# Layer 0 of a hybrid encoder: gated-convolution group first in the last weight piece, long convolution split between ScalarE and VectorE, short-convolution group in split products

## The chip, the cores and the metric

The kernel runs on one core of one Trainium2 chip. The metric is the device time of one execution in microseconds (us); the median of three runs is compared. The engines are named as the profile names them: PE (TensorE matmul), PEld (TensorE weight load), DVE (VectorE), ACT (ScalarE), POOL (GpSimd) and SP (SyncE, which issues nearly all the transfers).

## The reference, cut to what matters

Two layers over 256 positions with 2048 channels. Each layer normalises its input, modulates it with a scale and a shift that come from a conditioning row times `w_mod`, and multiplies by one wide matrix `w_in`. The columns of the product feed four head groups; their outputs go through `w_out`. A gated feed-forward follows. All is float32.

```python
h = layer_norm(x) * (1.0 + scale_m) + shift_m
proj = h @ w_in[l]                                     # 2048 x 4288
uv, q_c, kv_c, k_r, sb, sc, sh, ag = jnp.split(proj, IN_SPLITS, axis=-1)
y_a = gmlp_mixer(uv, ...)                              # U and V columns
y_b = mla_mixer(q_c, kv_c, k_r, ...)                   # B columns, attention
y_c = sb * causal_dwconv(sc * sh, sconv_w[l])          # E columns (sb), C columns (sc, sh), width 3
a, g = jnp.split(ag, 2, axis=-1)                       # D columns
y = causal_dwconv(a * sigmoid(g), conf_w_dw, conf_b_dw)   # width 31, per channel
y_d = silu(layer_norm(y, ...))
y = jnp.concatenate([y_a, y_b, y_c, y_d], axis=-1) @ w_out[l]
```

## The kernel before

**Storage.** Activations lie channel-major: four blocks of 128 channels by 256 positions make a tile of 128x1024. `hF` holds the modulated input of layer 0 in plain float32, one `slot` tile for every 4 of the 16 k-tiles. `hT` holds the same input split in two parts (high part and rest, `split`, L477 to L480), one tile of pool `act` (10 buffers) for every 2 k-tiles. In layer 0 `hT` exists for k-tiles 4 to 15 only (`PLAIN_KT` is 4).

**Products.** A product is either exact or split. Exact: the float32 weights are loaded straight into the split buffers (`wexact`, L438) and multiplied with `hF`; PE runs each such matmul as two instructions. Split: the weights go to a raw buffer (`wraw`, L446; pool `raw` has 4 buffers of 1 MB, used by the modulation weights `wmod` as well), ACT rounds them (`whi`, L460) and DVE subtracts (`wlo`, L461). `chan_major` and `group` then need three matmuls for each block of 128 output channels; `group2` (L533) needs two, one 512 wide (`whi` with both parts of the input) and one 256 wide (`wlo` with the high part).

**Layer 0.** `by_pieces` (L1271) goes over the k-tiles in five pieces, (0,2), (2,2), (4,4), (8,4), (12,4), because the modulation of a piece has to be there first. In each piece the work runs in four quarters: a quarter of D (1024 columns, four PSUM banks that stay open over all pieces, split products from k-tile 4 on), then U, then another quarter of D, V, D, E, D. U, V and E (512 columns each, exact) use two PSUM banks each per piece and are added to `sumU`, `sumV` and `sumE`, three tiles of pool `act`. After the last piece come `mix_d` (sigmoid and product, which starts the long convolution), `mix_u`, `gelu_v`, `mix_v`, then group B (704 columns, exact, `latent_group`), whose end is the attention (`mix_b`), then group C (1024 columns, exact, `group`), whose end is `mix_c`, the short convolution and `mix_e`. `out_proj` multiplies by `w_out`: the first 1024 columns split, the other two chunks of 512 exact.

**The long convolution** (`conv_d`, L890) is a list of 124 steps, one for each of four blocks and 31 taps: the first tap of a block on ACT, the other 30 as one DVE instruction each (L896: product with a tap and addition, up to 256 wide). The steps wait in `background`; `STEPS` says how many are issued with each unit of weights (7 with a unit of B, 8 with one of C). `norm_d` follows the last.

**The modulation stream.** `mods` (L338) yields 16 steps for each of ten rows of modulation, each a load of 1 MB of `w_mod` into a raw buffer and one DVE instruction 2048 wide (L240, the first of a row L238). `RATES` says how many steps are issued with each unit: 1.3 in B, 1.6 in C, 2.1 in `out_proj`. The first row (16 steps) is needed when the first chunk of `out_proj` ends; the second and third (48 steps in all) are needed inside its last chunk, before the second half of the positions.

**Order.** The framework's scheduler places the instructions of each engine when the kernel is built; program order is the priority, and an instruction whose operands or buffers aren't free yet lets later ones pass. At run time each engine goes through its list in order. Attention has a long chain of small steps, and PE works on C between them.

Of the kernel before, what the change touches and what calls it, by code (L numbers as in the profile page):

```python
# [7 lines left out]
F32 = mybir.dt.float32  # L8
F32R = mybir.dt.float32r
AF = mybir.ActivationFunctionType  # L10
ALU = mybir.AluOpType
# [21 lines left out]


RATES = [
    dict(B=1.3, C=1.6, out=2.1, up=0.7, down=0.7),
    dict(D=1.0, U=0.0, V=0.0, B=0.0, C=0.0, E=0.9, out=0.6, up=0.3, down=0.7),
]

STEPS = [  # L40
    dict(B=7, C=8, up=2),
    dict(U=7, B=4, C=4, E=8, up=2),
]

# [6 lines left out]
def encoder_kernel(ctx: ExitStack, tc: tile.TileContext, A: dict, consts: bass.AP, out: bass.AP):  # L51
# [321 lines left out]
    def phase(l, name):  # L373
        pace["rate"] = RATES[l][name]
# [470 lines left out]
    def mixers(l, w_in, Y, hF=None, between=None):  # L845
# [44 lines left out]
        def conv_d(glu):  # L890
            yd = slot("convD").rearrange("p (j s) -> p j s", j=4)
            def tap(j, k):
                if k == 30:
                    ident_act(yd[:, j, :], glu[:, j, :], CW(30, j), CB(j))
                else:
                    dve.scalar_tensor_tensor(  # L896
                        out=yd[:, j, 30 - k :],
                        in0=glu[:, j, : S - 30 + k],
                        scalar=CW(k, j),
                        in1=yd[:, j, 30 - k :],  # L900
                        op0=ALU.mult,
                        op1=ALU.add,
                    )

            for j in range(4):
                for k in range(30, -1, -1):
                    background.append(lambda j=j, k=k: tap(j, k))
            background.append(lambda: norm_d(yd))

        def norm_d(yd):  # L910
# [335 lines left out]
                dve.tensor_tensor(out=c, in0=c, in1=t, op=ALU.mult)  # L1246

        if hF is not None:
            return by_pieces(l, w_in, hF, between, mix_d, mix_u, gelu_v, mix_v, mix_b, mix_c, mix_e)
        phase(l, "V")  # L1250
        first_group(w_in, C_UV + 512, gelu_v)
        phase(l, "D")
# [15 lines left out]
        run(group2(w_in, C_SB, f"E{l}", joined_e, bg=STEPS[l]["E"]))  # L1268
        drain_background()

    def by_pieces(l, w_in, hF, between, mix_d, mix_u, gelu_v, mix_v, mix_b, mix_c, mix_e):  # L1271
# [8 lines left out]
        cols = {"U": C_UV, "V": C_UV + 512, "E": C_SB}  # L1280

        hT[:] = [None] * (PLAIN_KT // 2) + [act_pair("hT") for _ in range((KT - PLAIN_KT) // 2)]

        def terms(kt, part):

            hi, lo = part
            if lo is None:
                return [(hi, hf(kt))]
            xh, xl = (h[:, kt % 2, :] for h in hT[kt // 2][:2])
            return [(hi, xh), (hi, xl), (lo, xh)]  # L1290

        def chan_major(ps, kt, part, blocks, first, last):
            ts = terms(kt, part)
            for i in blocks:
                o = ps[i // 2][:, (i % 2) * S : (i % 2 + 1) * S]
                for n, (w, x) in enumerate(ts):
                    mm(o, w[:, i * P : (i + 1) * P], x, first and n == 0 and i % 2 == 0, last and n == len(ts) - 1)

        def side(g, parts, k0, nkt):
            ps = [acc_tile(f"{g}{l}_{i}") for i in range(2)]  # L1300
            for kt, part in parts:
                st, sp = kt == k0, kt == k0 + nkt - 1
                if g == "V":
                    ts = terms(kt, part)
                    for t in range(2):
                        for n, (w, x) in enumerate(ts):
                            mm(ps[t], x[:, t * P : (t + 1) * P], w, st and n == 0, sp and n == len(ts) - 1)
                else:
                    chan_major(ps, kt, part, range(4), st, sp)
            for i in range(2):  # L1310
                if k0 == 0:
                    act.copy(sums[g][i], ps[i])
                elif k0 + nkt == KT:
                    dve.tensor_tensor(out=sums[g][i], in0=ps[i], in1=sums[g][i], op=ALU.add)
                else:
                    part = tmp_tile("part")
                    act.copy(part, ps[i])
                    dve.tensor_tensor(out=sums[g][i], in0=part, in1=sums[g][i], op=ALU.add)

        first = between(0)[1]  # L1320
        first()
        for q, (k0, nkt) in enumerate(PIECES):
            ahead = between(q + 1) if q + 1 < len(PIECES) else ([], None)
            exact = k0 < PLAIN_KT
            loaded = {}

            def load(g, kt):

                c0, width = (C_AG, 1024) if g == "D" else (cols[g], 512)
                nk = min(2048 // width, nkt)  # L1330
                for j, p in enumerate(weights(w_in, kt, nk, c0, width, exact or g != "D")):
                    loaded[(g, kt + j)] = p

            mods_left = list(ahead[0])
            units = len(mods_left)

            def some_mods(share):
                while mods_left and (units - len(mods_left)) < units * share:
# [36 lines left out]
        run(group(w_in, C_SC, 1024, f"C{l}", mix_ce, hF=hf, bg=STEPS[l]["C"]))  # L1375
        drain_background()


# [253 lines left out]
```

## Time and profile before

| | |
|---|---|
| median of 3 runs | 2281.82 us (2278.19 to 2283.77) |
| the profiled execution | 2273.86 us |
| its span in the profile | 2271.7 us |
| mean granted PE clock | 0.992 |
| PE busy | 2206.6 us (97%) |
| DVE busy | 1792.9 us (79%) |
| ACT busy | 1060.8 us (47%) |
| data moved | 604.10 MB, mean 266 GB/s |

The times in the trace count from the start of the span. In layer 0 the last piece begins at about 157 us, B at 189.7, C has its first matmul at 230.3 and its last at 327.1, and `out_proj` runs from 327.1 to about 443. Layer 1 has its own B at 1292.6 and its own C, in two `group2` runs called Cc and Ch, from 1326.9 to 1402. A row of a list of groups gives the line, engine, operation, output and inputs, shapes and count, then the busy time and the mean of one, then the idle time of the engine ahead of it and what ended it. In a timeline merged rows count several instructions, and the time given reaches to the end of the last one, so the distance between instructions is read from the start of one row to the start of the next.

### The profile page before, as it was taken

What the parts mean: (1) busy time and instruction counts of PE and PEld (TensorE: products, weight loads), DVE (VectorE), ACT (ScalarE), POOL (GpSimd) and SP (SyncE); (2) the same over time, 40 slices, a digit from 0 to 9 for tenths busy, and PEclk for the clock granted to TensorE, in tenths of its full rate; (3) what the DMA queues carried; (4) which work ended last, traced back from release to release, by engine and by line L of the source; (5) the groups of instructions that cost most, each with busy time, mean ns of one, the idle gap of its engine ahead of it and who ended that gap; (6) DMA issues with size and microseconds to landing.
All of it is one profiled execution on the core that took longest, in us unless ns stands there. A gap on an engine that the chain in (4) does not pass through costs nothing. (4 is left out here: it accounts for less than half of the span.)

```text
span 2271.7 us, 28947 instructions
## 1 busy us (share of the span) xinstructions
PE 2206.6 (97%) x11118; PEld 1817.5 (80%) x11118; DVE 1792.9 (79%) x2282; ACT 1060.8 (47%) x1573; POOL 38.9 (2%) x61
## 2 busy tenths in 40 slices
PE   5899999999999999999999999999999999999998
PEld 4686786478888888887886888877888888888886
DVE  6878899588989898998977997878766565565676
ACT  2231241355554554544556544555555454454553
POOL 2000000000000000000000000000000000000000
PEclk9999999999999999999999999999999999999999
DMA  9999889879898989988975765876675555555553
GB/s 349 368 336 322 319 282 388 312 259 330 304 339 303 328 307 330 324 315 294 333 269 191 240 194 181 318 256 209 240 240 181 191 185 189 195 192 187 197 191 148
DMA packets 228658, 604.10 MB, mean 266 GB/s; under 512 B 14548, under 2 KB 27076, under 8 KB 206756
## 3 DMA queue, kind: packets, MB, share of 16 engines
q1 hardware_dynamic: 227672, 601.25, 75.0%
q8 instruction: 87, 1.43, 0.2%
q0 software_dynamic: 848, 1.01, 0.1%
q14 instruction: 51, 0.42, 0.1%
HBM read 600.11 MB, written 2.10 MB: 265 GB/s over the span
## 5 line engine op out<-in xcount | busy, mean ns | idle before, releaser
L461 DVE TENSOR_TENSOR wlo<-wraw,whi 128x1024 fp32r<-128x1024 f32 (+1 forms) x624 | 748.0, 1212 | 299.1 <-ACT whi L460 292.7
L460 ACT CAST whi<-wraw 128x1024 fp32r<-128x1024 f32 (+1 forms) x624 | 648.9, 1046 | 710.9 <-PE g_c L79 189.9
L79 PE MATMUL v_c<-hT,whi 128*128 128x512 f32 x1408 | 490.5, 392 | 0.0
L79 PE MATMUL g_c<-hT,whi 128*128 128x512 f32 x1280 | 445.6, 392 | 0.0
L79 PE MATMUL v_c<-hT,wlo 128*128 128x256 f32 x1408 | 393.9, 280 | 0.0
L79 PE MATMUL d<-whi,a 128*128 128x512 f32 x1344 | 386.8, 389 | 0.0
L240 DVE SCALAR_TENSOR_TENSOR macc<-wmod,cact,macc 128x2048 f32<-128x2048 f32 x150 | 351.6, 2344 | 17.0 <-DMA wmod<-in_w_mod_dram 16.2
L79 PE MATMUL g_c<-hT,wlo 128*128 128x256 f32 x1280 | 358.0, 280 | 0.0
L79 PEld LDWEIGHTS v_c<-hT,whi 128*128 128x128 f32 x1408 | 263.5, 187 | 58.8
L79 PEld LDWEIGHTS d<-whi,a 128*128 128x128 f32 x1344 | 252.1, 188 | 52.3
L79 PEld LDWEIGHTS g_c<-hT,whi 128*128 128x128 f32 x1280 | 239.5, 187 | 53.3
L79 PEld LDWEIGHTS v_c<-hT,wlo 128*128 128x128 f32 x1408 | 265.9, 189 | 0.2
L79 PEld LDWEIGHTS g_c<-hT,wlo 128*128 128x128 f32 x1280 | 241.7, 189 | 0.2
L79 PE MATMUL d<-wlo,a 128*128 128x512 f32 x672 | 233.2, 389 | 1.9 <-DVE wlo L461 1.9
L79 PEld LDWEIGHTS d<-wlo,a 128*128 128x128 f32 x672 | 126.1, 188 | 28.7 <-DVE wlo L461 2.7
L79 PE MATMUL o<-whi,a 128*128 128x512 f32 x352 | 101.1, 394 | 2.5 <-ACT whi L460 2.5
L896 DVE SCALAR_TENSOR_TENSOR convD<-gluD,pm,convD 128x255 f32<-128x255 f32 (+27 forms) x240 | 98.7, 456 | 0.4
L479 ACT CAST a<-g 128x512 fp32r<-128x512 f32 x132 | 81.1, 616 | 33.6 <-PE d L79 30.3
L480 DVE TENSOR_TENSOR a<-g,a 128x512 fp32r<-128x512 f32 x132 | 87.6, 683 | 1.8 <-ACT a L479 1.8
L604 PE MATMUL first<-wexact,hN 128*128 128x512 f32 x192 | 85.7, 596 | 1.5 <-ACT hN L82 1.2
L240 DVE SCALAR_TENSOR_TENSOR qacc<-wmod,cact,qacc 128x1024 f32<-128x1024 f32 (+1 forms) x75 | 80.2, 1070 | 2.4 <-DMA wmod<-in_w_mod_dram 0.4
L79 PEld LDWEIGHTS o<-whi,a 128*128 128x128 f32 x352 | 66.6, 190 | 17.1 <-ACT whi L460 2.9
(353 smaller groups left out, 2431.9 us busy)
## 6 DMA issues: line engine op xcount, KB each, us to landing
wraw<-in_ffn_w_up_dram SPq DMA_DIRECT2D x168, 1024.0 KB, 5.2
wmod<-in_w_mod_dram SPq DMA_DIRECT2D x160, 1024.0 KB, 6.9
wraw<-in_ffn_w_down_dram SPq DMA_DIRECT2D x88, 1024.0 KB, 5.2
wmod<-in_w_mod_dram SPq DMA_DIRECT2D x64, 512.0 KB, 8.8
wraw<-in_w_in_dram SPq DMA_DIRECT2D x30, 1024.0 KB, 6.5
wexact<-in_w_in_dram SPq DMA_DIRECT2D x52, 512.0 KB, 7.0
wraw<-in_w_out_dram SPq DMA_DIRECT2D x24, 1024.0 KB, 7.1
wexact<-in_w_out_dram SPq DMA_DIRECT2D x16, 512.0 KB, 11.4
```

The source lines that it names most:

```text
L79: pe.matmul(o, lhsT, rhs, start=start, stop=stop, skip_group_check=True)
L240: i = dve.scalar_tensor_tensor(out=acc, in0=w, scalar=col, in1=acc, op0=ALU.mult, op1=ALU.add)
L460: held(act.copy(hi[:, :m], r), "cast")
L461: i = dve.tensor_tensor(out=lo[:, :m], in0=r, in1=hi[:, :m].bitcast(F32), op=ALU.subtract)
L479: act.copy(hi, src)
L480: dve.tensor_tensor(out=lo, in0=src, in1=hi.bitcast(F32), op=ALU.subtract)
L604: i = pe.matmul(ps, hN[kt // 4][:, kt % 4, t * P : (t + 1) * P], parts[kt], start=kt == 0, stop=kt == KT - 1, skip_group_check=True,)
L896: dve.scalar_tensor_tensor(out=yd[:, j, 30 - k :], in0=glu[:, j, : S - 30 + k], scalar=CW(k, j), in1=yd[:, j, 30 - k :], op0=ALU.mult, op1 ...
```

## The change

In layer 0 alone: in the last piece all of D comes first, then `mix_d`, then U, V and E, with one step of a new rate `last` and five steps of the convolution behind each. A convolution step is now a whole tap: four ACT products 256 wide into one of two `scaled` tiles (pool `act`), and one DVE addition over all four blocks; 31 steps in place of 124, five behind each of U, V and E and one with each unit of B and C. `hT` is made for k-tiles 0 to 3 too, after `mix_v`. Group C becomes two `group2` runs of 512 columns (four units of 1 MB each) with layer 1's `first_c` (which adds the two halves of the PSUM banks into `chC`) and `second_c` behind them. `sumE` ends in a `slot` tile.

```diff
-    dict(B=1.3, C=1.6, out=2.1, up=0.7, down=0.7),
+    dict(last=1.0, B=1.3, C=1.4, out=2.0, up=0.7, down=0.7),
...
-    dict(B=7, C=8, up=2),
+    dict(last=5, B=1, C=1, up=2),
...
+            scaled = []
+
+            def taps(k):
+                if k == 30:
+                    for j in range(4):
+                        tap(j, k)
+                    return
+                if len(scaled) < 2:
+                    scaled.append(actp.tile([P, 1024], F32, tag="act", name="scaled").rearrange("p (j s) -> p j s", j=4))
+                t, n = scaled[(29 - k) % 2], S - 30 + k
+                for j in range(4):
+                    act.activation(out=t[:, j, :n], in_=glu[:, j, :n], func=AF.Copy, scale=CW(k, j))
+                dve.tensor_tensor(out=yd[:, :, 30 - k :], in0=yd[:, :, 30 - k :], in1=t[:, :, :n], op=ALU.add)
+
+            if hF is not None:
                 for k in range(30, -1, -1):
-                    background.append(lambda j=j, k=k: tap(j, k))
+                    background.append(lambda k=k: taps(k))
+            else:
+                for j in range(4):
+                    for k in range(30, -1, -1):
+                        background.append(lambda j=j, k=k: tap(j, k))
...
+                    if g == "E" and i == 0:
+                        whole = slot("sumE")
+                        ends[:] = [whole[:, j * 512 : (j + 1) * 512] for j in range(2)]
+                    dve.tensor_tensor(out=ends[i] if g == "E" else sums[g][i], in0=ps[i], in1=sums[g][i], op=ALU.add)
...
+            if q == len(PIECES) - 1:
+                for kt, h in turns_d:
+                    d_part(kt, h)
+                mix_d(accD, None)
+                phase(l, "last")
+                for g in "UVE":
+                    load(g, k0)
+                    side(g, [(kt, loaded[(g, kt)]) for kt in range(k0, k0 + nkt)], k0, nkt)
+                    pump()
+                    for _ in range(STEPS[l]["last"]):
+                        background.pop(0)()
+                continue
...
-        mix_d(accD, None)
         mix_u(sums["U"], None)
         for t in range(2):
             gelu_v(t, sums["V"][t])
         mix_v()
+        for i in range(PLAIN_KT // 2):
+            hT[i] = act_pair("hT")
+            split(hT[i], hF[i // 2][:, 2 * (i % 2) : 2 * (i % 2) + 2, :])
...
-        def mix_ce(cps, tps):
-            mix_c(cps, tps)
-            mix_e(sums["E"], None)
+        def mix_ce(cps):
+            second_c(cps)
+            mix_e(ends, None)
 
-        run(group(w_in, C_SC, 1024, f"C{l}", mix_ce, hF=hf, bg=STEPS[l]["C"]))
+        run(group2(w_in, C_SC, f"Cc{l}", first_c, bg=STEPS[l]["C"]))
+        run(group2(w_in, C_SC + 512, f"Ch{l}", mix_ce, bg=STEPS[l]["C"]))
```

More of the change, by code (lines that the diff above doesn't have):

```diff
@@ L903, in tap @@
                     )
-            for j in range(4):
-                for k in range(30, -1, -1):
-                    background.append(lambda j=j, k=k: tap(j, k))
+            scaled = []
[11 more added lines that the diff above has]
+            if hF is not None:
+                for k in range(30, -1, -1):
+                    background.append(lambda k=k: taps(k))
[3 more added lines that the diff above has]
+                        background.append(lambda j=j, k=k: tap(j, k))
             background.append(lambda: norm_d(yd))
@@ L1248, in mixers @@
         if hF is not None:
-            return by_pieces(l, w_in, hF, between, mix_d, mix_u, gelu_v, mix_v, mix_b, mix_c, mix_e)
+            return by_pieces(l, w_in, hF, between, mix_d, mix_u, gelu_v, mix_v, mix_b, first_c, second_c, mix_e)
         phase(l, "V")
@@ L1269, in mixers, with by_pieces @@
         drain_background()
-    def by_pieces(l, w_in, hF, between, mix_d, mix_u, gelu_v, mix_v, mix_b, mix_c, mix_e):
+    def by_pieces(l, w_in, hF, between, mix_d, mix_u, gelu_v, mix_v, mix_b, first_c, second_c, mix_e):
         hf = lambda kt: hF[kt // 4][:, kt % 4, :]
@@ L1280, in by_pieces @@
         cols = {"U": C_UV, "V": C_UV + 512, "E": C_SB}
+        ends = []
         hT[:] = [None] * (PLAIN_KT // 2) + [act_pair("hT") for _ in range((KT - PLAIN_KT) // 2)]
@@ L1313, in side @@
                 elif k0 + nkt == KT:
-                    dve.tensor_tensor(out=sums[g][i], in0=ps[i], in1=sums[g][i], op=ALU.add)
+                    if g == "E" and i == 0:
+                        whole = slot("sumE")
+                        ends[:] = [whole[:, j * 512 : (j + 1) * 512] for j in range(2)]
+                    dve.tensor_tensor(out=ends[i] if g == "E" else sums[g][i], in0=ps[i], in1=sums[g][i], op=ALU.add)
                 else:
```

## The prediction

> **What bounds the kernel now.** First the strips of the profile's page, for the place of the change: 40 slices of 56.8 us, in tenths. Layer 0's group work is slices 3 to 8.
>
> ```profile
> span 2271.7 us, 28947 instructions
> ...
> PE   5899999999999999999999999999999999999998
> ...
> DVE  6878899588989898998977997878766565565676
> ACT  2231241355554554544556544555555454454553
> ...
> DMA  9999889879898989988975765876675555555553
> ```
>
> PE is full from slice 2 on and ACT is the one idle engine there; DVE and the transfers are close behind PE. Strips can't say which of the three is last, so the second view is the table of stretches, cut where the stages change: last piece, B, attention with C, split part of the output projection, exact part.
>
> ```profile
> core 0: us, PE busy (x) PEld busy (x) DVE busy (x) ACT busy (x) POOL busy (x), PEclk, DMA share, GB/s
> 157.00:190.00 33.00, 33.00 (x184) 27.38 (x183) 17.84 (x15) 4.63 (x6) 0.00 (x0) 1.00 0.93 326
> 190.00:230.00 40.00, 39.60 (x143) 25.56 (x142) 37.97 (x72) 7.91 (x17) 1.92 (x2) 1.00 0.92 312
> 230.00:327.00 97.00, 92.67 (x431) 76.30 (x430) 87.14 (x145) 26.86 (x59) 4.64 (x4) 0.98 0.84 309
> 327.00:382.00 55.00, 50.90 (x227) 40.45 (x225) 50.33 (x47) 18.60 (x25) 0.00 (x0) 0.97 0.91 340
> 382.00:430.00 48.00, 47.35 (x129) 22.50 (x129) 31.39 (x26) 2.56 (x8) 0.00 (x0) 1.00 1.03 404
> sum 273.00, PE 263.51 PEld 192.20 DVE 224.67 ACT 60.57 POOL 6.55; mean PE 52.70 PEld 38.44 DVE 44.93 ACT 12.11 POOL 1.31
> ```
>
> PE misses 4.3 us of the 97 in the C stretch; DVE is at 95% in B and 90% with C, but at 54% in the last piece. So PE bounds, and DVE has its room in the wrong place. The Trainium skill warns of this reading ("Trainium Kernel Development and Optimization", Performance Expectations): matmul busy time is a bad measure, weight-load time a good one. By it PE would have slack (76.30 of 97 us), and fewer matmuls need save nothing (that outcome lies in the first rival). The distance of matmuls settles it; here C in layer 0, in the timeline and by tile, and layer 1's second half of C:
>
> ```profile
> 299.91 7.07 PE L79 MATMUL C_c<-hF,wexact 128*128 128x256 f32 x32
> 306.82 1.02 PE L79 MATMUL ps_gate<-macc,ones 128*128 128x512 f32 x2
> L79 PE MATMUL C_c<-hF,wexact x256: 379/379/634, 230.3 to 327.1; 128*128 128x256 f32 x128
> L79 PE MATMUL Ch_c<-hT,whi x64: 390/391/392, 1380.2 to 1402.0; 128*128 128x512 f32 x64
> L79 PE MATMUL Ch_c<-hT,wlo x64: 280/280/280, 1380.4 to 1402.3; 128*128 128x256 f32 x64
> ```
>
> 32 instructions take 306.82 - 299.91 = 6.91 us, one every 0.216 us with no gap: PE's own pace, so here its time is real. The split form takes (1402.0 - 1380.2) / 63 = 0.346 us for a pair, also without gaps.
>
> **The change part by part.**
>
> *C in split products (PE).* 16 k-tiles by 8 blocks are 128 products. Before: 256 x 0.216 = 55.3 us. After: 128 x 0.346 = 44.3 us. **-11.0 us** on the bounding engine, if the weights are there in time. D, U, V, E and B keep their matmuls; D first merely reorders them. D's last two k-tiles are wanted some 6 us into the piece; their buffers are no longer behind U's in the order, so I add nothing.
>
> *The cover.* C fills PE in the gaps of attention. In layer 0 it was exact and hung on nothing but a transfer; now it hangs on ACT and DVE. What that costs is shown by layer 1, where attention runs beside C in this very form:
>
> ```profile
> 1326.00:1380.00 54.00, 51.60 (x275) 42.53 (x274) 46.72 (x108) 26.33 (x60) 3.23 (x3) 1.00 0.48 156
> 1333.97 0.44 PE L1059 MATMUL ps_kv<-cst,lat 128*128 128x128 f32 x2 [2.19 <-ACT qg L1065]
> ```
>
> PE loses 2.4 us in 54 there, and the one gap of note is attention's own. But DVE is at 87% and the transfers at 0.48; layer 0 has 90% and 0.84. So the cover costs nothing as long as DVE and the raw buffers keep up, and these two are the question.
>
> *DVE.* Its rows between 157 and 327 us, and the distances:
>
> ```profile
> L240 DVE SCALAR_TENSOR_TENSOR macc<-wmod,cact,macc 128x2048 f32<-128x2048 f32 x25 | 58.5, 2341 | 9.1 <-DMA wmod<-in_w_mod_dram 9.1
> L896 DVE SCALAR_TENSOR_TENSOR convD<-gluD,pm,convD 128x235 f32<-128x235 f32 (+26 forms) x120 | 48.6, 453 | 0.1
> L480 DVE TENSOR_TENSOR hT<-hF,hT 128x512 fp32r<-128x512 f32 x2 | 1.3, 689 | 0.9 <-ACT hT L479 0.9
> L1104 DVE TENSOR_TENSOR rope<-ps_qr,qc 128x256 f32<-128x256 f32 x2 | 0.8, 420 | 0.2 <-PE ps_qr L79 0.2
> 210.54 5.85 DVE L896 SCALAR_TENSOR_TENSOR convD<-gluD,pm,convD 128x246 f32<-128x246 f32 x15
> 216.32 2.33 DVE L240 SCALAR_TENSOR_TENSOR macc<-wmod,cact,macc 128x2048 f32<-128x2048 f32 x1
> 349.13 2.35 DVE L461 TENSOR_TENSOR wlo<-wraw,whi 128x1024 fp32r<-128x1024 f32 x2
> 351.41 2.34 DVE L240 SCALAR_TENSOR_TENSOR macc<-wmod,cact,macc 128x2048 f32<-128x2048 f32 x1
> ```
>
> Removed: 120 tap instructions at (216.32 - 210.54) / 15 = 0.385 us, 46.2 us. Added: 30 additions. No row shows one; nearest is the 1024-wide two-tensor instruction, (351.41 - 349.13) / 2 = 1.14 us. The taps cover 4 x 225 to 4 x 255 elements, 6% less on average: I take 1.08, 32.4 us; the bounds are 30 x 0.69 (the 512-wide row) = 21 and 120 x 0.42 (256-wide pieces) = 50. Added too: 16 weight splits x 1.14 = 18.2; `hT` for four k-tiles, 1.3; joining the PSUM halves, 8 x 0.42 = 3.4. **Net +9.1 us.** From 157 to 382 us DVE is busy 193.3 of 225; after it has 202.4 for 214, 94.6%, just under the 37.97 of 40 that it reaches in B. So it fits only if the idle 15 us of the last piece get used. There I see a limit: `hT` (six), three sums and the first `scaled` fill the ten `act` buffers, so the second `scaled` waits until `sumU` is read. At 1.7 us of ACT for a tap (next row) only some seven of the 15 steps get done by 190 us, and the other eight, 9 us of DVE, fall into B, which is full.
>
> *ACT.*
>
> ```profile
> 329.73 1.70 ACT L1222 ACTIVATE yc<-chC,pm 128x256 f32<-128x256 f32 x4
> ```
>
> 30 taps x 1.70 = 51 us, and 16 rounding casts and some copies, some 20: 39 us busy of 170 become 110 of 159. It stays off the path. A page speaks against this part: the Trainium skill ("ScalarE: Activation LUTs", Rules for kernel authors) wants multiplications on VectorE. By it DVE would keep 46.2 instead of 32.4 us and need 216 of 214 us, so here the rule would cost 2 us; it compares two engines, not a full one with an idle one.
>
> *Raw buffers and the SP queue.* C's eight units of 1 MB now come through the four raw buffers that carry `wmod`. From 222 us until about 253 three of them hold attention's weights:
>
> ```profile
> 222.56 0.56 SPq L1026 DMA_DIRECT2D wkv<-in_mla_w_ukv_dram  x1
> ...
> 229.24 0.33 SPq L351 DMA_DIRECT2D wmod<-in_w_mod_dram  x1
> ...
> 238.61 0.33 SPq L351 DMA_DIRECT2D wmod<-in_w_mod_dram  x1
> ...
> 249.11 0.33 SPq L351 DMA_DIRECT2D wmod<-in_w_mod_dram  x1
> ...
> 253.63 4.00 SPq L351 DMA_DIRECT2D wmod<-in_w_mod_dram  x3
> ```
>
> The one left turns over every 10 us. Two units of C (11 us of PE work) are what PE used up to 263 us, and they come before most of these modulation steps, which then wait: two or three steps slip behind C, against 3 - 8 x 0.2 = 1.4 more issued ahead. A step that slips lands in the exact part of the projection, where the queues move 404 GB/s at a share of 1.03: 1.05 MB / 404 = 2.6 us each.
>
> **Sum.** -11.0 for PE, 0 to +8 for slipped steps and DVE in B and C (I take +3: one step more than the issue order gives back), 0 for ACT: **-8 us**. On the profiled execution 2273.86 - 8 = 2266; on the median of the runs, 8 us higher, **2274 us**. A measurement of this kernel tells about 0.3% (6.8 us) from no change.
>
> **The rivals.**
>
> 1. *Given back.* DVE is the bound from 190 to 316 us. With eight taps left over from the last piece and 18 us of splits it needs some 128 of 126 us, and the steps of modulation that run ahead now (27 in this window, where 23 were due) slip by three or four: 8 to 10 us, of which the exact part can take little. -11 + 5..11 = -6..0. For it: 94.6% over all. Against it: DVE is idle 16 us of the 48 after 382.
>
> 2. *Slower through the raw buffers.* Eight turns go from the modulation to C. If all eight steps end up behind 382 us, they add 8 x 2.6 = 20.8 us to a stretch that is full, and the end of the projection moves by -11 + 20.8 = +10 us: 2292. It decides from the fifth slipped step on (11.0 / 2.6 = 4.2). For it: the one free buffer, and the share of 1.03. Against it: after 253 us all four buffers turn, and 91 MB in 262 us are 349 GB/s, below 404:
>
> ```profile
> DMA packets 24742, 91.35 MB, mean 335 GB/s; under 512 B 3537, under 2 KB 5124, under 8 KB 18328
> ```
>
> The Trainium skill ("DMA: Bandwidth & Descriptors", Specifications) gives a core some 358 GB/s of HBM. By it the 91 MB need 255 us, and nothing could be caught up. The 404 GB/s over 48 us say otherwise, so it adds little to this rival.
>
> 3. *More than forecast.* The filler comes in smaller pieces, DVE's attention steps meet fewer conv steps (16 or so instead of 120 from B on), and PE's own gaps shrink too:
>
> ```profile
> 237.48 0.64 PE L1059 MATMUL ps_q<-cst,lat 128*64 128x128 f32 x2 [2.54 <-ACT qg L1068]
> 279.11 0.30 PE L1174 MATMUL ps_pT<-cst,p 128*128 128x128 f32 x1 [1.64 <-DVE p L1165]
> ```
>
> Then -11 - 4 = -15: 2267.
>
> **How the numbers follow.** Forecast (-7 to -12) 0.42; more than forecast 0.10; given back (-6 to +6) 0.27; slower 0.21, most of it +7 to +13. Faster 0.52, same 0.27, slower 0.21. The unknown cost of the 1024-wide additions (21 to 50 us of DVE) is held in rivals 3 and 1. The range runs from 2265 (all of rival 3 and 2 us of drift) to 2291 (the mass of rival 2 up to its price), with about 2 in 10 outside. Likeliest case alone: 2270 to 2275.
>
> **What would show it right or wrong.** In the changed profile: `Cc` and `Ch` pairs 0.346 us apart, and PE's work of C at 44 us; the last matmul of C at about 316 to 319 us; DVE at 94% or more between 190 and 316; the 48th step before 416 us; from the feed-forward on the same distances as before. Rival 1 shows as idle time of PE ahead of `Cc`, `Ch` or the projection, ended by DVE `wlo` or ACT `whi`; rival 2 as PE waiting in the exact part for `wexact` or for the sums of `macc`. I am wrong if the additions take much more than 1.1 us, if D first leaves PE without weights at 163 us, or if ACT's products delay attention's chain.

## The result and the profile after

The changed kernel takes 2296.76 us (median of five runs, 2295.45 to 2299.56); the kernel before, run beside it, 2283.77 us. The ratio is 1.0061, with a 95% interval of 1.0043 to 1.0078: 13 us slower, where 8 us faster was forecast. The time lies above the range as well.

The strips of the profile's page for the changed kernel, 40 slices of 57.3 us:

```profile
span 2293.7 us, 29079 instructions
...
PE   5899888999999999999999999999999999999998
...
DVE  6877898678899889998977987887676565665676
ACT  2236652164555454544556545556455455454453
...
DMA  9997789958888998998875755876765556555554
```

Counted from 0, as in the prediction's "full from slice 2 on", PE has three slices of 8 there now (4 to 6), and the transfers fall to 7 in slices 3 and 4. ACT has its new work. The table of stretches, cut where the stages change in this kernel (last piece, B, C with attention, split part of the projection, exact part), with one row over the first four:

```profile
core 0: us, PE busy (x) PEld busy (x) DVE busy (x) ACT busy (x) POOL busy (x), PEclk, DMA share, GB/s
157.00:193.40 36.40, 33.88 (x189) 27.95 (x188) 19.66 (x19) 12.82 (x22) 0.00 (x0) 1.00 0.79 279
193.40:234.00 40.60, 40.17 (x146) 25.75 (x144) 39.61 (x44) 33.09 (x81) 4.12 (x2) 1.00 0.70 244
234.00:330.20 96.20, 83.73 (x430) 67.54 (x430) 85.05 (x94) 56.77 (x121) 7.08 (x4) 0.95 0.83 293
330.20:397.80 67.60, 55.49 (x228) 43.06 (x227) 60.09 (x58) 21.75 (x29) 0.19 (x1) 0.90 0.90 338
397.80:460.00 62.20, 62.02 (x161) 29.67 (x159) 38.89 (x51) 5.92 (x17) 1.55 (x2) 0.95 0.91 359
...
157.00:397.80 240.80, 213.27 (x986) 164.30 (x985) 204.41 (x213) 124.43 (x250) 11.38 (x6) 0.95 0.82 295
```

Two rows carry the result. With C, PE is busy 83.7 us instead of 92.7, but the stretch is as long as before (96.2 against 97): PE's idle time there went from 4.3 to 12.5 us. And the split part of the projection, which the change doesn't touch, takes 67.6 us instead of 55.6 (327.1 to 382.7). The last piece is 3.7 us longer (36.4 against 32.7).

The first feed-forward matmul starts at 462.5 us, before at 444.5; the rest of the two spans differs by 4 us more. The profiled execution of before was 8 to 10 us under the medians of its kernel, so of the 22 us between the two spans some 9 belong to that one execution. In what follows I use the time from the first matmul of B to the first of the feed-forward, which every profile has: 254.8 us before, 269.1 after.

### The profile page after: what moved, and what is told of

Its sections match the earlier page's. It is cut to its first block, busy times and chain, and to the rows that moved or that the text cites. A ratio compares the mean times of both kernels' runs of the same rounds, so it can differ in the third digit from the quotient of the medians.

```text
span 2293.7 us, 29079 instructions
## 1 busy us (share of the span) xinstructions
PE 2211.2 (96%) x11118; PEld 1815.7 (79%) x11118; DVE 1802.4 (79%) x2218; ACT 1127.5 (49%) x1717; POOL 42.8 (2%) x61
## 3 DMA queue, kind: packets, MB, share of 16 engines
q0 software_dynamic: 848, 1.01, 0.1%
## 5 line engine op out<-in xcount | busy, mean ns | idle before, releaser
L460 ACT CAST whi<-wraw 128x1024 fp32r<-128x1024 f32 (+1 forms) x640 | 665.5, 1045 | 739.2 <-PE g_c L79 204.1
L461 DVE TENSOR_TENSOR wlo<-wraw,whi 128x1024 fp32r<-128x1024 f32 (+1 forms) x640 | 768.0, 1215 | 300.2 <-ACT whi L460 294.4
L1458 DVE SCALAR_TENSOR_TENSOR u<-g,pf,u 128x254 f32<-128x254 f32 (+1 forms) x176 | 73.7, 480 | 0.3 <-ACT u L82 0.2
```

Source lines behind the costliest of these rows:

```text
L460: held(act.copy(hi[:, :m], r), "cast")
L461: i = dve.tensor_tensor(out=lo[:, :m], in0=r, in1=hi[:, :m].bitcast(F32), op=ALU.subtract)
L1458: dve.scalar_tensor_tensor(out=u[:, sh:], in0=x[:, : S - sh], scalar=col(k, j), in1=u[:, sh:], op0=ALU.mult, op1=ALU.add)
```

## The experiments

First the theories. **S**: C in split products is by itself too dear in layer 0. **J**: the second `scaled` tile jams ACT. **D**: D first costs the time. J has a row for it, in the timeline of ACT:

```profile
193.87 1.70 ACT L916 ACTIVATE scaled<-gluD,pm 128x254 f32<-128x254 f32 x4 [12.20 <-DVE sumE L1336]
```

ACT stands 12.2 us for the buffer that the sum of E leaves, so one addition gets done before 190 us.

**e1: `sumE` in a slot from the start,** so that the second `scaled` tile need not wait for it.

```diff
-            both = actp.tile([P, 1024], F32, tag="act", name=f"sum{g}")
+            both = slot("sumE") if g == "E" else actp.tile([P, 1024], F32, tag="act", name=f"sum{g}")
```

> The changed kernel with one buffer more for the long convolution: sumE lies in a slot tile from the start, so the second scaled tile no longer waits for it. Theory J (jam): in the changed kernel the second scaled tile got sumE's buffer, so 28 of the 30 additions came after 193.9 us, filled VectorE in B, held the modulation back in the raw buffers, and the first weights of C and of attention were issued some 20 us late. Then this run has some 6 additions before the end of the last piece, less than 5 us of idle PE between 233 and 264 us (the changed kernel: 9.8), and ends 8 to 16 us below the changed kernel, -5 to +3 us to the kernel before. Theory S (split C is too dear in layer 0, whatever the convolution does): it stays +8 to +14 us above the kernel before, with PE waiting ahead of Cc and Ch as in the changed kernel.

Measured: 2296.39 us, ratio to before 1.0068 [1.0042, 1.0094]. J falls: the wait is gone, seven additions are begun before B, and the time stays.

**e2: the kernel before with C in split products alone.**

```diff
-        run(group(w_in, C_SC, 1024, f"C{l}", mix_ce, hF=hf, bg=STEPS[l]["C"]))
+        run(group2(w_in, C_SC, f"Cc{l}", first_c, bg=STEPS[l]["C"]))
+        run(group2(w_in, C_SC + 512, f"Ch{l}", mix_ce, bg=STEPS[l]["C"]))
```

> The kernel before with group C in split products alone (hT for all k-tiles, sumE in a slot tile so that hT fits); the convolution, the last piece and the rates stay. Theory J: no jam; PE saves up to 11 us in C, VectorE has 23 us more to do and gives some back: -6 to +3 us to the kernel before. Theory S: +8 us or more, PE idle ahead of Cc and Ch more than 10 us, and the first Cc weights issued no earlier than in the changed kernel (235 us).

Measured: 2300.13 us, 1.0085 [1.0060, 1.0111]. That is S's time, but not its signs: C's first weights are issued at 215.5 us, not at 235, and PE is idle 7.4 us with C, not over 10.

**e3: the changed kernel with C exact** (D first and the new convolution alone); the reverse of the diff of e2.

> The changed kernel with group C exact as before (no hT for k-tiles 0 to 3, no weight splits in C): D first and the new convolution alone. Theory J: the second scaled tile still waits for sumE, VectorE is full from 194 to 240 us, attention's weights are issued after 230 us (before: 216 to 222), and the time is +3 to +10 us. Theory S: without split C there is nothing to lose; -3 to +2 us.

Measured: 2278.68 us, 0.9989 [0.9974, 1.0004].

**e4: the kernel before with D first alone.**

> The kernel before with D first in the last piece and the gated product right behind it, and nothing else (124 convolution steps as before, no extra modulation steps). In the changed kernel B began 3.7 us late (193.4 against 189.7 us), with one stop of PE of 2.5 us at 160 us. Theory D (D first costs this by itself): B begins at 192 us or later and the time is +3 to +6 us. Theories J and S: B begins late only because of the convolution's share; 0 to +2 us.

Measured: 2281.68 us, 1.0001 [0.9987, 1.0015]. D's first sign is there: B begins at 196.0 us, and from D's first matmul to B the last piece takes 39.2 us against 35.1 before. But the whole is not slower. So D falls as the cause of the loss and S stands: everything that is lost comes with the split form of C. The stretches of C and of the split projection in e2:

```profile
233.60:323.60 90.00, 82.61 (x413) 66.80 (x412) 85.53 (x133) 36.18 (x70) 2.07 (x3) 0.96 0.78 278
323.60:406.20 82.60, 62.39 (x246) 49.56 (x245) 72.96 (x82) 23.66 (x33) 0.70 (x1) 0.79 0.86 318
```

C is 7 us shorter than before and the projection 27 us longer. Why, was the next question: VectorE's work (**V**), the raw buffers (**R**), or the clock after PE's stops (**K**).

**e5: the changed kernel without its 30 paired taps.**

```diff
                     for j in range(4):
                         tap(j, k)
                     return
+                return
```

> The changed kernel without its 30 paired conv additions and without the ScalarE products that feed them (the conv's convolution then has one tap, k = 30, so this part of the computation is left out); the weight splits of C, their raw buffers and the order stay. DVE loses about 30 x 1.08 = 32 us, ACT 51 us. Theory V (VectorE is the bound from B to the end of the split projection, and the splits of C are what overfills it): C and the projection end 20 us earlier or more than in the changed kernel, and PE, at its 44 us for C, keeps the forecast gain: -6 to -15 against the kernel before. Theory R (the eight units of C hold the raw buffers, and weights and modulation come late whatever VectorE does): +5 to +13, as in the changed kernel.

Measured: 2284.76 us, 1.0014 [1.0003, 1.0026].

```profile
233.30:317.50 84.20, 81.27 (x431) 66.08 (x430) 62.36 (x75) 38.88 (x75) 4.19 (x4) 1.00 0.79 282
317.50:388.60 71.10, 57.63 (x227) 44.92 (x227) 61.20 (x58) 21.71 (x29) 0.14 (x1) 0.86 0.90 333
```

Neither theory had this. With some 32 us less on DVE, C is 12.8 us shorter than before: the forecast gain of PE is there. And the projection takes 71.1 us, 15.5 longer than before, with DVE at 86%.

**e6: C's weights without their low part.**

```diff
-            i = dve.tensor_tensor(out=lo[:, :m], in0=r, in1=hi[:, :m].bitcast(F32), op=ALU.subtract)
+            if high:
+                lo = hi
```

> The changed kernel where C's weights get no low part: the 16 subtractions of C are left out and the high part is multiplied in both matmuls (the low product of C is wrong by that). PE has the same instructions; DVE loses 16 x 1.14 = 18 us; a raw buffer comes free after ACT's cast alone. Theory V: -8 to +3 against the kernel before, with the split projection ending by 385 us. Theory R: the buffers' turns get shorter by one subtraction only, +6 to +12. If the stops of PE behind ACT's cast (the clock then falls) are what counts (theory K), it stays above +5 as well, with stops ended by ACT whi and a granted clock under 0.95 in the C stretch.

Measured: 2295.77 us, 1.0065 [1.0050, 1.0080]. Eighteen microseconds of DVE bring nothing, against V; the 15 us are more than R's range and fit K. C stays at 96.7 us at a granted clock of 0.93, with stops of 2.1, 2.2 and 4.3 us behind ACT at its begin, as in the changed kernel.

**e7: C's raw weights through slot tiles, not raw buffers.**

```diff
-            r = raw[:, k * width : k * width + m]
+            if by_slots:
+                r = slot("wslot")
+                nc.sync.dma_start(
+                    out=r.rearrange("p (k c) -> p k c", k=per),
+                    in_=w[(k0 + k) * P : (k0 + k + per) * P, c0 : c0 + width].rearrange("(k p) c -> p k c", p=P),
+                )
```

> The changed kernel with C's raw weights in two 0.5 MB tiles of the ordinary weight slots for each unit, so that the four raw buffers stay with the modulation, as before the change. DVE, ACT and PE have the same instructions. Theory R: modulation steps are back at 27 by the end of C and the time falls to +3 or less against the kernel before. Theory V: no difference to the changed kernel worth the name, +8 to +14, VectorE over 90% busy from B to the end of the split projection.

Measured: 2303.01 us, 1.0092 [1.0071, 1.0113]. The projection is back at 55.3 us, as before the change; but C takes 119, because its loads wait for slots on SP and the modulation steps, let loose, stand in front of attention's small DVE steps. PE stops for 5.4, 7.2 and 4.0 us there, each time until DVE has finished attention's `p`.

The time meets neither expectation, so as a test of the raw buffers by the time it fails; its projection is the first sign that they matter.

**e8: the first half of C exact, the second split.**

```diff
-        run(group2(w_in, C_SC, f"Cc{l}", first_c, bg=STEPS[l]["C"]))
+        run(group(w_in, C_SC, 512, f"Cc{l}", first_x, nk=4, hF=hf, bg=STEPS[l]["C"]))
```

> The changed kernel with the first half of C exact (as before the change) and only the second half in split products. PE gains 5.5 us instead of 11; DVE gets 9 us of splits instead of 18. Theory V: the sum of VectorE's work between B and the end of the split projection is then below what it was before, so this gains, -6 to 0 against the kernel before. Theory K (each stop of PE in front of a split unit costs clock as well): between the exact version (-3) and the changed kernel (+13), so +3 to +7.

Measured: 2291.27 us, 1.0044 [1.0026, 1.0061]. C is 5.7 us shorter than before (91.3), the projection 13 longer (68.6). Half the splits cost over two thirds of the whole. That is against V, and 10 us are above K's range as well.

**What the profiles have in common.** The queue of SP shows it. The loads of the projection's split weights in the kernel before, where C ends at 327.1, and in the changed kernel, where it ends at 330.2:

```profile
289.11 0.38 SPq L446 DMA_DIRECT2D wraw<-in_w_out_dram  x1
303.47 0.38 SPq L446 DMA_DIRECT2D wraw<-in_w_out_dram  x1
313.70 0.38 SPq L446 DMA_DIRECT2D wraw<-in_w_out_dram  x1
```

```profile
305.88 0.38 SPq L446 DMA_DIRECT2D wraw<-in_w_in_dram  x1
312.40 0.38 SPq L446 DMA_DIRECT2D wraw<-in_w_out_dram  x1
320.91 0.38 SPq L446 DMA_DIRECT2D wraw<-in_w_out_dram  x1
336.45 0.38 SPq L446 DMA_DIRECT2D wraw<-in_w_out_dram  x1
```

Before, three of the projection's eight units are on their way when C ends, the third 13 us ahead. After, C's own last unit passes first (305.88) in the same four buffers, and the third unit of the projection is issued 6 us too late. Over all 20 profiles, experiments still to come included:

| units issued before C ends | kernels | split part of the projection |
|---|---|---|
| 2 | after, e1, e2, e5, e6, e8, e12, e16 | 67 to 83 us |
| 3 | before, e3, e4, e10, e11, e14, e15, e17, e18 | 51 to 60 us |
| 4 or 5 | e7, e9, e13 | 44 to 56 us |

There is no overlap between the first row and the others. The next runs ask what makes the third unit late: bytes (**T**), or turns of the buffers, DVE's share in each among them (**U**). Each edit was made in both kernels, and the pairs are compared; a pair's interval is worked out from the two (root of the sum of squares).

**e9 and e10: half the bytes of modulation,** DVE's work as before.

```diff
-                nc.sync.dma_start(out=raw, in_=A["w_mod"][l, kt * P : (kt + 1) * P, m * D : (m + 1) * D])
+                nc.sync.dma_start(out=raw[:, :1024], in_=A["w_mod"][l, kt * P : (kt + 1) * P, m * D : m * D + 1024])
...
-                mod_step(acc, raw, kt, kt == 0)
+                for h in range(2):
+                    mod_step(acc[:, h * 1024 : (h + 1) * 1024], raw[:, :1024], kt, kt == 0)
```

> The kernel before, where each modulation step of the stream loads only the left half of its weights (0.5 MB instead of 1 MB) and VectorE uses that half twice, in two instructions of 1024 (the right halves of the modulation vectors are wrong by that). The turns of the raw buffers and VectorE's work stay, the bytes of modulation are halved, about 24 MB less by the 48th step. Only the pair with the next run counts. Theory T (what is left of the loss is bytes: the stretch up to the exact part moves what the queues can carry): before gets faster by 5 to 20 us.

> The same edit in the changed kernel. Theory T: with the bytes gone, PE's gain can be cashed, and this run is faster than its partner by 4 to 11 us, where the full kernels stand 13 us apart the other way. Theory U (not the bytes but the turns: a raw buffer is held until VectorE has used it, and eight more of them pass through the four): still 8 us or more slower than its partner, with VectorE over 90% busy from B to the end of the split projection.

Measured: 2276.16 us (0.9981 [0.9967, 0.9994]) and 2294.32 us (1.0068 [1.0045, 1.0090]). The pair stands 0.87% apart, give or take 0.26: no better than the full kernels. T as a single cause falls. But the stretches tell more than the time; C and the split projection of e10:

```profile
234.10:331.80 97.70, 86.55 (x433) 69.81 (x431) 86.76 (x112) 55.89 (x119) 5.20 (x4) 0.93 0.64 214
331.80:390.00 58.20, 50.81 (x223) 39.57 (x222) 55.71 (x65) 20.61 (x28) 0.00 (x0) 0.97 0.85 293
```

The projection has come down from 67.6 to 58.2 us, the third unit now 8 us ahead. C is as long as ever, with DVE at 89%.

**e11 and e12: half of DVE's work in the modulation,** all its bytes.

```diff
-                mod_step(acc, raw, kt, kt == 0)
+                n = D if kt == 0 else D // 2
+                mod_step(acc[:, :n], raw[:, :n], kt, kt == 0)
```

> The kernel before, where each modulation step of the stream but the first of a vector loads its whole 1 MB but VectorE adds up only the left half of it (the right halves of the modulation vectors are left at their first step). Bytes and turns stay, a raw buffer comes free 1.1 us sooner, VectorE loses about 1.1 us for each of 45 steps. Only the pair with the next run counts. Theory T: within 5 us of the kernel before.

> The same edit in the changed kernel. Theory U: with VectorE down by 40 us or more between 157 and 400 us its partner is caught up or passed, 0 to -11 us beside it. Theory T: still 5 us or more behind its partner, with the split projection at 65 us or longer and the transfer share at 0.9 there.

Measured: 2277.63 us (0.9987 [0.9974, 1.0000]) and 2288.31 us (1.0032 [1.0020, 1.0045]); apart 0.45%, give or take 0.18. U's number is missed and T's are hit, though e10 had just spoken against T. C and the split projection of e12:

```profile
239.00:326.80 87.80, 83.72 (x431) 68.98 (x432) 64.94 (x94) 51.95 (x110) 2.33 (x4) 0.96 0.84 296
326.80:396.20 69.40, 57.16 (x227) 44.56 (x226) 48.70 (x57) 21.62 (x29) 0.00 (x0) 0.85 0.89 341
```

The mirror image: C has its gain, 10 us shorter than its partner's 98.1, and the projection is as bad as ever although DVE is busy only 70% of it.

**e13 and e14: both halves at once.** Theory **W**: two limits in two places, DVE with C and the loads ahead of the projection. Theory **X**: neither.

```diff
-                mod_step(acc, raw, kt, kt == 0)
+                for h in range(2 if kt == 0 else 1):
+                    mod_step(acc[:, h * 1024 : (h + 1) * 1024], raw[:, :1024], kt, kt == 0)
```

> The kernel before with both halvings at once: each modulation step loads only the left half of its weights, and VectorE adds up only that half (the right halves of the modulation vectors are wrong by that). Only the pair with the next run counts.

> The same edit in the changed kernel: VectorE has some 40 us more room between 157 and 400 us, and the transfers some 24 MB. Theory W (two limits of nearly the same height stand behind TensorE, VectorE and the transfers; relieving one leaves the other): PE's gain now comes out, and this run is faster than its partner by 4 to 11 us. Theory X (neither; the split weights themselves are late, because a split needs two tiles where an exact weight needs one, and the buffers so hold half as many units ahead): still 4 us or more slower than its partner.

Measured: 2272.02 us (0.9962 [0.9951, 0.9973]) and 2269.15 us (0.9953 [0.9937, 0.9970]). The pair is level: -0.09%, give or take 0.20, that is -2 us, from -7 to +3.

```profile
238.70:326.00 87.30, 83.97 (x433) 69.33 (x432) 64.43 (x95) 52.21 (x110) 3.26 (x4) 0.96 0.65 219
326.00:377.50 51.50, 49.67 (x226) 40.54 (x225) 41.47 (x51) 20.41 (x28) 0.00 (x0) 0.97 0.76 260
```

Both places are good here at once, as nowhere else, and 15 us of the difference are gone. From B to the feed-forward e14 is 4.0 us shorter than e13 (244.3 against 248.3). The full 11 us don't come out, since the partner gains as well: its projection takes 43.8 us with five units ahead. W stands, and of its forecast the lower edge at best. X falls: the number of split tiles is as in the changed kernel, and the pair is level.

**e15: the new long convolution alone,** C exact and D in its old place, `STEPS` with B=2 and C=1.

> The kernel before with the new long conv alone (ScalarE products and 30 wide additions on VectorE): C exact, D in its old place, the sums in their old tiles. VectorE gets 46.2 - 32.4 = 14 us of room between 190 and 330 us and PE nothing. If room on VectorE is worth something by itself there: -3 to -8 us. If it is worth something only together with a shorter PE: 0, within 3 us. Beside the run of D first with exact C (-3) it tells what D first costs.

Measured: 2277.60 us, 0.9983 [0.9973, 0.9993]: 4 us faster than before. It is the only one of the versions that do the whole work whose interval leaves out no change on the fast side, though by less than the 0.3% of the forecast's bound.

**e16: the kernel before with three raw buffers.**

```diff
-    rawp = ctx.enter_context(tc.tile_pool(name="rawp", bufs=4))
+    rawp = ctx.enter_context(tc.tile_pool(name="rawp", bufs=3))
```

> The kernel before with three raw buffers instead of four, and nothing else. If the turns of the raw buffers are a limit of the stretch from B to the exact part (theory U), a quarter of them gone makes it slower by 10 us or more over the whole kernel, with the modulation behind at 327 us and a split projection over 60 us. If the buffers have room (theory X or W): under 5 us.

Measured: 2338.03 us, 1.0244 [1.0223, 1.0264], 56 us slower over both layers, 19 of them between B and the feed-forward of layer 0. U's signs are all there. C stays exact, and still the split projection looks as it does in the changed kernel:

```profile
337.50:409.60 72.10, 57.97 (x226) 43.95 (x225) 58.43 (x52) 19.02 (x25) 0.00 (x0) 0.88 0.86 310
```

Here too the third unit comes late, 3.7 us after C. So a lack of raw buffers alone makes the long projection, without a single split in C. The opposite, a fifth raw buffer in the changed kernel, wasn't tried.

**e17: as e10, but two half steps share one turn of a raw buffer.**

```diff
+                if kt % 2 == 0:
+                    raw = raw_tile("wmod")
+                    for h in range(2):
+                        nc.sync.dma_start(
+                            out=raw[:, h * 1024 : (h + 1) * 1024],
+                            in_=A["w_mod"][l, (kt + h) * P : (kt + h + 1) * P, m * D : m * D + 1024],
+                        )
+                    for k in (kt, kt + 1):
+                        for h in range(2):
+                            mod_step(acc[:, h * 1024 : (h + 1) * 1024], raw[:, (k - kt) * 1024 : (k - kt + 1) * 1024], k, k == 0)
```

> The changed kernel with half the bytes of modulation, as in e10, but with the halves of two steps side by side in one raw buffer and used right after each other: the same bytes and the same work on VectorE as e10, and half as many turns of the raw buffers for modulation (some 17 fewer between 190 and 400 us). Theory U (the turns themselves): 10 us or more faster than e10, near the kernel before halved alike (-4). Theory W (a turn costs only the transfer and the VectorE work that it carries): within 5 us of e10, +11 to +20.

Measured: 2285.11 us, 1.0014 [1.0000, 1.0028], 0.54% less than e10, give or take 0.27: some 9 us by the medians and 12 by the ratios, at the same bytes and the same work of DVE. U's number is met at its edge and W's is missed: turns seem to have a price of their own. The edit also brings the two steps together in the order, every second time instead of one by one, and no run separates that from the turns. In the profiles about 6 us of it lie between B and the feed-forward (252.3 against 258.5; the third unit 13 us ahead instead of 8); where the rest is saved I can't say, since the edit reaches the later modulation as well.

**e18: e15 with rates set to the room that it leaves.**

```diff
-    dict(B=1.3, C=1.6, out=2.1, up=0.7, down=0.7),
+    dict(B=1.5, C=1.9, out=1.7, up=0.7, down=0.7),
```

> The new long conv alone (as e15) with the rates of modulation set to the room that it leaves: 1.5 in B, 1.9 in C and 1.7 in the split projection, where e15 has 1.3, 1.6 and 2.1. VectorE was busy 76.7 of 93 us with C and the transfers at 0.86. If the room can be used, some three steps come before the projection and its split part gets 4 to 8 us shorter: -6 to -10 against the kernel before. If the raw buffers allow no more turns there: as e15, -2 to -5.

Measured: 2281.02 us, 0.9994 [0.9983, 1.0005]: neither expectation. When C ends, 29 modulation steps are begun, against 27 in e15, whose C ends 6 us earlier; by 327 us it is 28 against 27. So the higher rates bring one or two steps where three were expected. The split part is 2 us shorter than in e15 (53.6 against 55.6), the exact part up to the feed-forward 4.5 us longer (67.6 against 63.1), and the gain of e15 is gone. What three more steps ahead would bring isn't shown.

## Why the prediction was wrong, point by point

**C in split products: right in size.** In the second half of C, PE's pairs are as far apart as forecast; in the timeline of the changed kernel, the starts 8 pairs apart:

```profile
316.23 0.39 PE L79 MATMUL Ch_c<-hT,whi 128*128 128x512 f32 x1
...
319.01 0.39 PE L79 MATMUL Ch_c<-hT,whi 128*128 128x512 f32 x1
```

2.78 / 8 = 0.347 us. Where DVE had room (e5, e12, e14), C did become 10 to 13 us shorter than before or than in the partner.

**DVE: the amount right, its place wrong.** 202.4 us were forecast from 157 us to the end of the split projection, and 204.4 were measured; the additions cost 1.01 to 1.13 us from one start to the next, where 1.08 was taken. But "202.4 for 214, 94.6%" set a sum against a sum. In B, DVE is busy 39.6 of 40.6 us with 18 of the 30 additions and the modulation steps between them. The loads ahead of C stand on SP until such steps have left their raw buffers: 13 us in all from 205 to 236 us, against 5 before. Here are SP's queue and PE's stops at the begin of C:

```profile
220.04 11.98 SPq L351 DMA_DIRECT2D wmod<-in_w_mod_dram  x4
235.01 0.38 SPq L446 DMA_DIRECT2D wraw<-in_w_in_dram  x1
```

```profile
236.24 0.33 PE L1077 MATMUL ps_q<-cst,lat 128*128 128x128 f32 x1 [2.08 <-ACT lat L1062]
238.74 0.95 PE L1077 MATMUL ps_q<-cst,lat 128*128 128x128 f32 x3 [2.17 <-ACT junk L1055]
245.05 2.08 PE L79 MATMUL Cc_c<-hT,whi 128*128 128x512 f32 x4 [4.33 <-ACT whi L460]
```

C's first unit is issued after B has ended, and its first product comes at 245 us, where before it came at 230.3. So nothing fills attention's first gaps, and 8.6 of the 12.5 us that PE is idle with C lie here. In e5, without the additions, the same unit is issued at 215.8 us, and PE's idle time with C is 2.9 us.

**"So the cover costs nothing as long as DVE and the raw buffers keep up":** this is the step that failed, in its condition. It was carried by layer 1, where transfers are at a share of 0.48; e10 and e12 show that in layer 0 neither half of the condition holds.

**Raw buffers: the slip right, the price wrong.** Two or three modulation steps were to slip behind C. It was three (24 instead of 27 done at 327 us), and the 48th began at 434 us instead of 417. The price was put at 2.6 us each, in the exact part, by bytes. That part is only 2 to 3 us longer. What I left out is that the projection's own units come through the same four buffers and the same in-order queue: the second of them slipped by 17 us and the third by 23, and the bill is the 12 us in the split projection. The term "I take +3" came to about +24 (11 of gain not cashed, 13 lost).

**The clock: not in the sum at all.** PE's timeline at D first and around the worst stop in the projection:

```profile
160.39 1.11 PE L79 MATMUL D_c<-hT,whi 128*128 128x256 f32 x5 [2.52 <-ACT hT L479]
...
342.57 1.22 PE L79 MATMUL o<-wlo,a 128*128 128x512 f32 x2 [4.97 <-DVE wlo L461]
343.59 1.91 PE L79 MATMUL o<-whi,a 128*128 128x512 f32 x4
345.29 1.05 PE L79 MATMUL o<-wlo,a 128*128 128x512 f32 x2
346.15 1.06 PE L79 MATMUL o<-whi,a 128*128 128x512 f32 x2
347.00 0.81 PE L79 MATMUL o<-wlo,a 128*128 128x512 f32 x2
347.65 1.09 PE L79 MATMUL o<-whi,a 128*128 128x512 f32 x4
348.57 0.62 PE L79 MATMUL o<-wlo,a 128*128 128x512 f32 x2
```

Right after the stop four matmuls take 345.29 - 343.59 = 1.70 us, 5 us after it 0.92. The 12 matmuls from 342.57 to 347.65 take 5.1 us, 2.3 more than at 0.23 us each. So PE pays for a stop again, by about half its length. The same work costs it 55.5 us in the projection instead of 50.8, at a granted clock of 0.90 instead of 0.97: of the 12 us, some 7 are idle time and some 5 slow matmuls, which is theory K's share. By the Trainium skill ("TensorE: Matmul & The Clock Gate", Part 1) the clock is halved after an idle window of some 3.4 us. The trace agrees for this stop (0.425 us a matmul against 0.23); in the last piece a stop of 2.52 us leaves the granted clock at 1.00. In e4 a stop of only 2.08 us at the same place is followed by 3.4 us at 0.53, so here the length of the stop alone doesn't decide.

The stop itself is ended by DVE, whose list has the end of the short convolution in front of the projection's split. ACT's casts stand behind the end of C as well:

```profile
336.93 3.25 DVE L1242 SCALAR_TENSOR_TENSOR yc<-chC,pm,yc 128x254 f32<-128x254 f32 x8
340.08 1.30 DVE L1254 TENSOR_TENSOR yc<-yc,sumE 128x512 f32<-128x512 f32 x2
341.29 2.37 DVE L461 TENSOR_TENSOR wlo<-wraw,whi 128x1024 fp32r<-128x1024 f32 x2
```

```profile
335.05 1.04 ACT L460 CAST whi<-wraw 128x1024 fp32r<-128x1024 f32 x1
...
342.69 1.99 ACT L460 CAST whi<-wraw 128x1024 fp32r<-128x1024 f32 x2 [0.60 <-DMA wraw<-in_w_out_dram]
...
382.82 2.00 ACT L460 CAST whi<-wraw 128x1024 fp32r<-128x1024 f32 x2 [8.98 <-DMA wraw<-in_w_out_dram]
```

Each unit is cast in two halves. The first unit's were done at 319.78 and 321.17, the one at 335.05 is the second unit's, so it is the second unit that PE waits for in this stop, not the third: issued at 320.91 instead of 303.47, it fell behind the end of C on both lists. The third is cast at 342.69, as soon as it has landed, so PE would have stood for it next; how the stop divides between the two isn't shown. The later stop of 3.1 us, at 383.92, is ended by the cast at 382.82, which waited for its transfer. The kernel before has the same end of C at 332 to 337 us without a stop: by 330 us DVE had split two units there, 48 matmuls or 11 us of PE's work from 327.1 on, and the next split begins at 336.60. So the count of three units in the table above is a sign of how far the loads are ahead, not what each stop waits for.

**The second `scaled` tile:** one addition instead of seven before 190 us, since its buffer came from the sum of E, not of U. It cost nothing (e1). **D first:** nothing over the whole (e4), but the term that the prediction put at nothing in the last piece is 3 to 4 us: 2.5 of them are the stop at 160.39, where D waits not for weights but for the split input of its last k-tiles (ACT `hT`). **ACT:** nothing found on the path from the products themselves; e3 and e15 have them and aren't slower. The rule of the Trainium skill ("ScalarE: Activation LUTs", Rules for kernel authors) that the prediction weighed, multiplications on VectorE, isn't borne out here as to the time: with 120 products on ACT e15 is 4 us faster, on an engine that had room. One instruction for another, the trace does not speak against it: a product is 0.42 us on ACT (1.70 for four) and a product with its addition 0.385 on DVE.

**The rivals.** Rival 1 (DVE gives the gain back) is what happens in the C stretch. Rival 2 gave 2292 and the sign; its resource is right by e16, its place wrong: not bytes in the exact part but the buffers ahead of the split part, and three slipped modulation steps were enough where it asked for five. It should have had more than 0.21. I took the two as alternatives, and they came together, in two stretches. Rival 3 had nothing.

**What stays open:** whether and why a turn of a raw buffer has a price of its own, what part of the 15 us that e14 recovers is bytes and what part turns, and how the worst stop in the projection divides between the second unit's late split and the third unit's late landing.

## What to carry to other kernels

Work that is moved from a plentiful buffer to a scarce one delays whatever uses the scarce one next, in a stage that the change doesn't touch: list the stage's first loads and see when each is issued. Take two nearly full resources as two bills that may fall due in different stretches, not as one maximum; relieving either alone then shows little in the total, so read an experiment by stretches. A saving on the bounding engine is worth what its followers can already have in flight.

## What the runs showed of the hardware that wasn't expected

A stop of PE of 5 us costs some 2.3 us more in slow matmuls behind it (0.425 us each against 0.23, back to pace 5 us after the stop), and stretches with several stops run at a granted clock of 0.79 to 0.90 (e2, the projection of the changed kernel, e5). After stops of 2.52 us (changed kernel) and 2.08 us (e4) at the same place, the clock stayed at 1.00 in the one and fell to 0.53 in the other. Two transfers of 0.5 MB into one raw buffer, used right after each other, were 9 to 12 us cheaper over the kernel than the same two in two buffers (e10, e17; the order of the steps changed with it). One raw buffer of four was worth 56 us.
